# Inverting the 32-row triangles of a chunked RWKV-7 scan as two blocks of 16 at once, joined by small matmuls

## The chip, the core and the metric

The kernel is one program on one core of a Trainium2 chip. The core has five engines that run side by side, each through its own list of instructions in order: TensorE (PE, with its weight loads shown apart as PEld), VectorE (DVE), ScalarE (ACT), GpSimd (POOL) and SyncE (SP, which issues the DMAs). They wait for one another by semaphores. The metric is the device time of one execution in microseconds (us). The granted clock of TensorE is shown as a share of full speed; 1.00 is 2.4 GHz and 0.50 is 1.2 GHz.

## The reference, cut to what matters

One step of a two-layer backbone on 640 tokens (128 of a prompt, 512 of a grid) with 1024 channels. Each layer has a large input projection, an RWKV-7 branch, a gated MLP branch, an output projection and a feed-forward block. The RWKV-7 branch is a recurrence over tokens, for 16 heads of 64 channels in two directions:

```
def _rwkv_step(S, inp):
    r, w, k, v, neg_kk, b = inp
    sa = jnp.einsum('dbhij,dbhj->dbhi', S, neg_kk)
    S = S * w[..., None, :] + sa[..., :, None] * b[..., None, :] + v[..., :, None] * k[..., None, :]
    return S, jnp.einsum('dbhij,dbhj->dbhi', S, r)
```

The kernel does not step through tokens. It cuts them into 10 chunks of 64 and, within a chunk, needs the inverse of a unit triangular matrix of 64 rows whose entries are products of `neg_kk` and `b` with the decays between them. With that inverse a chunk is a handful of matmuls, and only the state goes from chunk to chunk.

## The kernel before, in words

Channels lie on partitions, tokens along the free axis. Every dense product is taken in three fp32r passes (high by high, high by low, low by high), each weight block being loaded as `raw`, rounded to `hi` by ScalarE (line 101) and subtracted to `lo` by VectorE (line 103). A dense block of 128 output channels is 48 matmuls of 128x320 in line 111; the profile counts each of them once, and each fp32 matmul twice (two passes).

Heads are handled in pairs, 8 pairs per layer (`NPAIR`), and each pair in two generators. `front(i)` prepares pair i: decays and scaled operands (`LA`, `BK`, called the scaling part below), then 40 gram matmuls `g` (line 644) whose results are copied out by ScalarE and VectorE, then 20 transposes of `BK` (line 664), then the triangular inverses, then the join of two 32-row halves to 64 rows. `back(i)` runs the chunks of pair i: 22 transposes `trv` (line 730), then 10 chunk steps of matmuls into `pu` (lines 751 to 795). While `back(i)` runs, `front(i+1)` is advanced between its steps: the table `SP['n']` says by how many yields after each of the 10 chunk steps. Dense blocks for pair i+2 (`krv_block`) and for the gates (`gate_block`) are put in between as well. The front of pair 0 has no back beside it. A scheduler then places every instruction by its own estimates and by the priorities (`high_priority`), so that the order on an engine mixes all of these.

The inverses, before: a 64-row triangle has two diagonal triangles of 32 rows. Tile `D` holds them with heads and halves on four groups of 32 partitions (quadrants) and 20 units (10 chunks, two directions) along the free axis. A 32x32 VectorE transpose (line 668) puts one triangle on each partition, as `AA`. POOL makes the unit triangle `X` of it by two selections (lines 670, 671). Then 30 steps of forward substitution follow on VectorE, each a product into scratch (line 676, written over `D`) and a sum into `X` (line 678) over (31-s)*s elements. Two transposes (lines 692, 694) give the inverse in both orientations, `XT` and `XN`; four ScalarE copies (line 698) put it into `TT`. Two groups of 40 quadrant matmuls, `pw` in lines 705 and 715, with ScalarE copies behind them (lines 709, 718), form the 32x32 block off the diagonal. `back(i)` reads `TT` in line 789.

Of the kernel before, what the change touches and what calls it, by code (L numbers as in the profile page):

```python
# [16 lines left out]
T = TP + TS  # L17
# [17 lines left out]
SP = {'n': (3, 2, 1, 2, 2, 1, 0, 0, 3, 1), 'v': 1, 'k': 4, 'r': 7, 'kk': 7, 'F': 200, 'B': None, 't': 10, 'g0': 2, 'gn': (2, 2, 2, 1, 2, 2, 2, 1)}  # L35
# [6 lines left out]
def emit(tc, I, O, depth=DEPTH, mark=lambda s: None):  # L42
    nc = tc.nc
    ctx = ExitStack()
    with ctx:
# [22 lines left out]
        for half in range(2):  # L68
# [4 lines left out]
            nc.gpsimd.affine_select(m_str[s], m_str[s], pattern=[[1, L]], compare_op=ALU.is_gt, fill=0.0, base=0, channel_multiplier=-1)  # L73
        cb = {}
# [19 lines left out]
        def dense_ps():  # L94
            return psd.tile([128, 2, 512], F32, tag="d", name="dps")
# [211 lines left out]
        for l in range(depth):  # L307
# [73 lines left out]
            with tc.tile_pool(name=f"com{l}", bufs=1) as com:  # L381
# [139 lines left out]
                with tc.tile_pool(name=f"rw{l}", bufs=1) as rw:  # L521
# [25 lines left out]

                    st_ = {}
# [33 lines left out]
                    def front(i):  # L582
# [87 lines left out]
                        nc.gpsimd.affine_select(X, AA, pattern=[[1, 32], [-1, 32]], compare_op=ALU.is_gt, fill=0.0, base=0, channel_multiplier=0)  # L670
                        nc.gpsimd.affine_select(X, X, pattern=[[1, 32], [-1, 32]], compare_op=ALU.not_equal, fill=1.0, base=0, channel_multiplier=0)  # L671
                        tm = D.rearrange("p u t -> p (u t)")
                        for s in range(1, 31):
                            n = 31 - s
                            t3 = tm[:, 0:n * s].rearrange("p (a b) -> p a b", b=s)
                            nc.vector.tensor_tensor(t3, AA[:, s + 1:32, s:s + 1].to_broadcast([128, n, s]),  # L676
                                                    X[:, s:s + 1, 0:s].to_broadcast([128, n, s]), ALU.mult)
                            nc.vector.tensor_tensor(X[:, s + 1:32, 0:s], X[:, s + 1:32, 0:s], t3, ALU.add)  # L678
                            if s % 5 == 0:
                                yield "sub"  # L680
                            if s == 10:
# [12 lines left out]
                        nc.vector.transpose(XN.rearrange("p u j -> p j u"), X.rearrange("p t j -> p j t"))
                        for q in range(4):
                            s = slice(32 * q, 32 * q + 32)
                            o = 32 * (q % 2)
                            nc.scalar.activation(TT[s, :, o:o + 32], XT[s, 0:20, :], AF.Copy)
# [379 lines left out]
```

## Time and profile before

| what | us |
|---|---|
| median of 3 runs (lowest, highest) | 3382.55 (3381.95, 3396.24) |
| the profiled execution | 3388.05 |
| its span, first to last instruction | 3386.3 |
| TensorE matmuls busy | 3159.4 (93%) |
| VectorE busy | 2145.6 (63%) |
| ScalarE busy | 1511.6 (45%) |
| GpSimd busy | 612.4 (18%) |

Per engine, busy time is the union of its instructions' times. Matmuls overlap in the array and their ends are modelled, so a busy TensorE is not one at its peak: a row with few, short matmuls at half clock is also counted as busy. A line of the kind `L676 DVE ... x480 | 178.1, 371 | 21.6 <-POOL X L671 11.7` says: line 676 on VectorE, 480 times, 178.1 us busy, 371 ns for one, 21.6 us of idle time just before them, most of it ended by GpSimd's line 671. The pairs' part of the program stands at about 300 to 1100 us (layer 0) and 1960 to 2770 us (layer 1).

### The profile page before, as it was taken

How to read it: one execution, taken by the hardware profiler on the slowest of the kernel's cores; microseconds unless marked ns; L12 is line 12 of the kernel's file. 1: busy time of each engine (PE TensorE's matmuls, PEld its weight loads, DVE VectorE, ACT ScalarE, POOL GpSimd, SP SyncE). 2: the span in 40 equal slices, each digit the busy share in tenths (PEclk: the TensorE clock that was granted, in tenths of full speed). 3: DMA queues.
4: the chain of work that ended last, by engine and by line, in shares of the span. 5: the costliest groups of instructions: out<-in, count | busy, mean ns of one | idle time of the engine just before them, and what ended most of it. 6: DMA issues, size and time to landing. Idle time of an engine off the chain costs nothing.

```text
span 3386.3 us, 66312 instructions
## 1 busy us (share of the span) xinstructions
PE 3159.4 (93%) x26160; PEld 2862.3 (85%) x26160; DVE 2145.6 (63%) x4147; ACT 1511.6 (45%) x3268; POOL 612.4 (18%) x616
## 2 busy tenths in 40 slices
PE   7998899999999999999989979999999999999998
PEld 7897677777778989999989967777777789899998
DVE  7777778887785469933353487788787735532234
ACT  5444445554445354224254434445544543541432
POOL 3004333333231000000000133333323210000000
PEclk8998889998899999999999989899889999999999
DMA  6683112221224536622344522122222245222223
GB/s 210 220 291 102 56 61 72 77 74 61 66 77 138 199 104 205 216 83 75 99 135 139 188 75 66 56 73 77 68 68 72 86 137 184 84 76 75 75 75 106
DMA packets 215671, 372.73 MB, mean 110 GB/s; under 512 B 63680, under 2 KB 72000, under 8 KB 215360
## 3 DMA queue, kind: packets, MB, share of 16 engines
q1 hardware_dynamic: 215360, 368.49, 33.8%
q8 instruction: 206, 3.38, 0.4%
q14 instruction: 105, 0.86, 0.1%
HBM read 288.41 MB, written 63.31 MB: 104 GB/s over the span
## 4 chain that ended last, share of the span: by engine, by line
PE 65%; DVE 18%; DMA 5%; issue 5%; ACT 4%; POOL 3%; SPq 1%; DVEq 0%; ACTq 0%; POOLq 0%
PE dps L111 40%; PE g L644 4%; DMA wada<-in_wada 3%; PE dps L256 3%; PE dps L491 2%; DVE X L678 2%; DVE D L676 2%; PE pu L776 2%; DVE wjunk L168 2%; PE pu L757 2%; PE pu L789 1%; PE pu L795 1%; PE pu L751 1%; DVE lo L103 1%; POOL BK L625 1%
## 5 line engine op out<-in xcount | busy, mean ns | idle before, releaser
L101 ACT ACTIVATE hi<-raw 128x512 fp32r<-128x512 f32 x630 | 397.2, 632 | 1025.6 <-PE dps L111 864.0
L103 DVE TENSOR_TENSOR lo<-raw,hi 128x512 fp32r<-128x512 f32 x550 | 392.1, 714 | 545.9 <-ACT hi L101 526.7
L111 PE MATMUL dps<-ah,hi 128*128 128x320 f32 x2768 | 686.9, 324 | 8.4 <-ACT up L468 5.4
L111 PE MATMUL dps<-ah,lo 128*128 128x320 f32 x2768 | 674.3, 321 | 14.5 <-DVE lo L103 14.5
L111 PE MATMUL dps<-al,hi 128*128 128x320 f32 x2768 | 674.9, 321 | 0.0
L111 PEld LDWEIGHTS dps<-ah,lo 128*128 128x128 f32 x2768 | 474.4, 193 | 29.5 <-DVE lo L103 16.5
L111 PEld LDWEIGHTS dps<-ah,hi 128*128 128x128 f32 x2768 | 474.2, 192 | 28.2 <-ACT up L468 6.0
L111 PEld LDWEIGHTS dps<-al,hi 128*128 128x128 f32 x2768 | 473.9, 192 | 12.7 <-issue 0.8
L168 DVE CUSTOM_DVE_ANT_0 wjunk<-wada,sc 128x1024 f32<-128x1024 f32 x176 | 220.9, 1255 | 33.2 <-DMA wada<-in_wada 30.9
L785 POOL TENSOR_TENSOR sw<-SV,wc 64x128 f32<-64x128 f32 x288 | 150.7, 523 | 439.0 <-DVE SV L803 422.5
L644 PE MATMUL g<-LA,BK 64*128 64x128 f32 x1280 | 193.6, 332 | 32.9 <-DVE LA L656 15.9
L103 POOL TENSOR_TENSOR lo<-raw,hi 128x512 fp32r<-128x512 f32 x80 | 123.2, 1540 | 543.6 <-ACT hi L101 491.8
L644 PEld LDWEIGHTS g<-LA,BK 64*128 64x128 f32 x1280 | 162.0, 226 | 64.6 <-issue 22.2
L111 PE MATMUL dps<-fh,lo 128*128 128x320 f32 x896 | 205.5, 311 | 6.2 <-DVE lo L103 6.0
L111 PE MATMUL dps<-fh,hi 128*128 128x320 f32 x896 | 204.7, 310 | 0.0
L111 PE MATMUL dps<-fl,hi 128*128 128x320 f32 x896 | 204.5, 309 | 0.0
L676 DVE TENSOR_TENSOR D<-AA,X 128x30 f32<-128x30 f32 (+14 forms) x480 | 178.1, 371 | 21.6 <-POOL X L671 11.7
L678 DVE TENSOR_TENSOR X<-X,D 128x30 f32<-128x30 f32 (+14 forms) x480 | 179.9, 375 | 11.3
L249 POOL TENSOR_TENSOR al<-nt,ah 128x320 fp32r<-128x320 f32 x24 | 25.2, 1053 | 728.1 <-ACT ah L248 727.0
L111 PEld LDWEIGHTS dps<-fh,lo 128*128 128x128 f32 x896 | 150.0, 188 | 7.9 <-DVE lo L103 7.8
L625 POOL TENSOR_TENSOR BK<-ta,cum 64x640 f32<-64x640 f32 x64 | 125.8, 1966 | 141.4 <-DVE ta L616 116.3
L111 PEld LDWEIGHTS dps<-fh,hi 128*128 128x128 f32 x896 | 150.3, 188 | 0.0
(293 smaller groups left out, 5798.1 us busy)
## 6 DMA issues: line engine op xcount, KB each, us to landing
raw<-in_w SPq DMA_DIRECT2D x280, 256.0 KB, 2.6
raw<-in_win SPq DMA_DIRECT2D x234, 256.0 KB, 2.7
wada<-in_wada SPq DMA_DIRECT2D x88, 512.0 KB, 4.1
ld<-up SPq DMA_DIRECT2D x80, 320.0 KB, 3.6
th<-ld SPq DMA_DIRECT2D x32, 320.0 KB, 2.9
ta<-ld SPq DMA_DIRECT2D x32, 320.0 KB, 3.0
gd<-spill SPq DMA_DIRECT2D x32, 320.0 KB, 2.3
raw<-in_wo SPq DMA_DIRECT2D x40, 256.0 KB, 2.6
```

Source lines behind the costliest of these rows:

```text
L101: nc.scalar.activation(hi, raw, AF.Copy)
L103: (eng or nc.vector).tensor_tensor(lo, raw, hi.bitcast(F32), ALU.subtract)
L111: nc.tensor.matmul(ps[:, n, 0:HT], w[:, k * 128:(k + 1) * 128], xk[:, n * HT:(n + 1) * HT], start=(first and k == 0 and j == 0), stop=(las ...
L168: nc.vector.tensor_tensor_reduce(junk, wt, sc_cur[0][:, v, :], 1.0, 0.0, ALU.mult, ALU.add, mods[l][:, j, v:v + 1])
L256: nc.tensor.matmul(ps[:, n, 0:HT], w[:, k * 128:(k + 1) * 128], x[:, 4 * kb + k, hs(n)], start=(kb == 0 and k == 0 and j == 0), stop=(kb = ...
L491: nc.tensor.matmul(o, x[:, k, tk * 128:(tk + 1) * 128], w[:, kk * 256:(kk + 1) * 256], start=(k == 0 and j == 0 and tk % 2 == 0), stop=(k ...
L625: nc.gpsimd.tensor_tensor(b[s, c, 1 - h, :], rt[s], e[s], ALU.mult)
L644: nc.tensor.matmul(gs[h][:, c - c0, :], b[s, c, :, :].rearrange("p x t -> p (x t)"), la[s, c, h:h + 2, :].rearrange("p x t -> p (x t)"), s ...
L676: nc.vector.tensor_tensor(t3, AA[:, s + 1:32, s:s + 1].to_broadcast([128, n, s]), X[:, s:s + 1, 0:s].to_broadcast([128, n, s]), ALU.mult)
L678: nc.vector.tensor_tensor(X[:, s + 1:32, 0:s], X[:, s + 1:32, 0:s], t3, ALU.add)
L757: nc.tensor.matmul(pu[s, d, 3, :], SV[:, us[d], h, :], GR[d][:, cs[d], h, :], start=False, stop=True, skip_group_check=True)
L785: nc.gpsimd.tensor_tensor(sw[s], SV[s, both, h, :], wcu[s, both].unsqueeze(2).to_broadcast([64, 2, L]), ALU.mult)
```

## The change

`X` becomes the triangle with its lower left 16x16 block cleared, so that its two diagonal blocks of 16 rows can be inverted side by side: a view `xb` with a dimension for the block lets one VectorE instruction work on both, and the steps run to 14 instead of 30. `X` is transposed into as before (`AA` is gone), and the scratch is a tile `tm` of its own.

The cleared block is then brought in by TensorE. `pwa` multiplies the whole triangle `D` with the first 16 columns of the inverse (80 quadrant matmuls of 32x16). VectorE masks the result to rows 16 to 31 (`low16`) and adds the identity, into `wq`, whose other 16 columns are a constant identity. Multiplying with `wq` on one side gives the inverse in one orientation, `pwt` (80 matmuls of 32x32), and on the other side in the other, `pwn` (40, two quadrants only). ScalarE copies `pwn` into `XN` and `pwt` into `TT` (twelve copies in place of four). The join to 64 rows follows as before, reading `TT` instead of `XT`. The front's yields become fewer, the table `SP['n']` follows, the `bon` part moves behind the steps, and a memory reservation is made smaller.

```
-SP = {'n': (3, 2, 1, 2, 2, 1, 0, 0, 3, 1), ...
+SP = {'n': (3, 2, 1, 2, 2, 1, 1, 1, 1, 1), ...
+        idq = G([128, 32], "idq")
+        for q in range(4):
+            nc.vector.tensor_copy(idq[32 * q:32 * q + 32, :], ident[32 * q:32 * q + 32, 32 * q:32 * q + 32])
+        low16 = G([128, 1], "low16")
+        nc.vector.tensor_reduce(low16, idq[:, 16:32], mybir.AxisListType.X, ALU.add)
...
+                    wq = rw.tile([128, 20, 32], F32, tag="wq", name="wq")
+                    nc.gpsimd.tensor_copy(wq[:, :, 16:32], idq[:, 16:32].unsqueeze(1).to_broadcast([128, 20, 16]))
...
-                        AA = rw.tile([128, 32, 32], F32, tag="s4", name="AA", bufs=3)
-                        nc.vector.transpose(AA, D.rearrange("p u t -> p t u"))
-                        X = rw.tile([128, 32, 32], F32, tag="s4", name="X", bufs=3)
...
-                        tm = D.rearrange("p u t -> p (u t)")
-                        for s in range(1, 31):
-                            n = 31 - s
-                            t3 = tm[:, 0:n * s].rearrange("p (a b) -> p a b", b=s)
-                            nc.vector.tensor_tensor(t3, AA[:, s + 1:32, s:s + 1].to_broadcast([128, n, s]),
-                                                    X[:, s:s + 1, 0:s].to_broadcast([128, n, s]), ALU.mult)
-                            nc.vector.tensor_tensor(X[:, s + 1:32, 0:s], X[:, s + 1:32, 0:s], t3, ALU.add)
-                            if s % 5 == 0:
+                        X = rw.tile([128, 33, 32], F32, tag="sX", name="X")
+                        xf = X.rearrange("p t s -> p (t s)")
+                        xa = X[:, 0:32, :]
+                        nc.vector.transpose(xa, D.rearrange("p u t -> p t u"))
+                        nc.gpsimd.memset(xa[:, 16:32, 0:16], 0.0)
...
+                        xb = xf.rearrange("p (a r) -> p a r", a=2)[:, :, 0:512].rearrange("p a (t s) -> p a t s", s=32)
+                        tm = rw.tile([128, 128], F32, tag="tm", name="tm")
+                        for s in range(1, 15):
+                            n = 15 - s
+                            t4 = tm[:, 0:2 * n * s].rearrange("p (a t s) -> p a t s", a=2, s=s)
+                            nc.vector.tensor_tensor(t4, xb[:, :, s + 1:16, s:s + 1].to_broadcast([128, 2, n, s]),
+                                                    xb[:, :, s:s + 1, 0:s].to_broadcast([128, 2, n, s]), ALU.mult)
+                            nc.vector.tensor_tensor(xb[:, :, s + 1:16, 0:s], xb[:, :, s + 1:16, 0:s], t4, ALU.add)
+                            if s % 7 == 0:
                                 yield "sub"
...
+                        quads = [slice(32 * q, 32 * q + 32) for q in range(4)]
+                        pw = psr.tile([128, 20, 16], F32, tag="g", name="pwa")
+                        for u in range(20):
+                            for s in quads:
+                                nc.tensor.matmul(pw[s, u, :], D[s, u, :], XN[s, u, 0:16], start=True, stop=True)
+                        nc.vector.scalar_tensor_tensor(wq[:, :, 0:16], pw, low16, idq[:, 0:16].unsqueeze(1).to_broadcast([128, 20, 16]), ALU.mult, ALU.add)
+                        yield "W"
+                        for x in range(2):
+                            us = slice(10 * x, 10 * x + 10)
+                            pt = psr.tile([128, 10, 32], F32, tag="g", name="pwt")
+                            pn = psr.tile([128, 10, 32], F32, tag="g", name="pwn")
+                            for u in range(10 * x, 10 * x + 10):
+                                for s in quads:
+                                    nc.tensor.matmul(pt[s, u - 10 * x, :], wq[s, u, :], XT[s, u, :], start=True, stop=True)
+                            for u in range(10 * x, 10 * x + 10):
+                                for s in quads[0::2]:
+                                    nc.tensor.matmul(pn[s, u - 10 * x, :], XT[s, u, :], wq[s, u, :], start=True, stop=True)
+                            for s in quads[0::2]:
+                                nc.scalar.activation(XN[s, us, :], pn[s], AF.Copy)
+                            for q, s in enumerate(quads):
+                                o = 32 * (q % 2)
+                                nc.scalar.activation(TT[s, us, o:o + 32], pt[s], AF.Copy)
+                        yield "V"
...
+    nc = _bacc.Bacc("TRN2", target_bir_lowering=False, num_devices=1, dynamic_dma_scratch_size=2048)
```

The new steps move instructions on every engine. Three places follow, before and then after. In these rows `dps` is a dense block (after the change its line is 116), `pu` a chunk step of `back`, `pg` and `trv` as above; a row's `x40` counts matmuls of the program, of which the trace shows two records each.

TensorE, layer 0, the join of the front of pair 0, before:

```order
L111 MATMUL dps<-ah,hi 128x320 x2
L111 MATMUL dps<-al,hi 128x320 x2
L111 MATMUL dps<-ah,lo 128x320 x2
L705 MATMUL pw<-XN,TT_2827 32x32 x40
L715 MATMUL pw_3237<-XT,XN 32x32 x20
L715 MATMUL pw_3238<-XT,XN 32x32 x20
L730 MATMUL trv<-ident,vp_2547 128x128 x4
```

And after:

```order
L116 MATMUL dps<-ah,lo 128x320 x2
L116 MATMUL dps<-ah,hi 128x320
L709 MATMUL pwa<-XN,D 32x16 x80
L116 MATMUL dps<-ah,hi 128x320
L116 MATMUL dps<-al,hi 128x320 x2
L116 MATMUL dps<-ah,lo 128x320 x2
L718 MATMUL pwt<-XT,wq 32x32 x40
L721 MATMUL pwn<-wq,XT 32x32 x20
L586 MATMUL pg<-kksq,ones_b 128x320 x2
L718 MATMUL pwt<-XT,wq 32x32 x40
L721 MATMUL pwn<-wq,XT 32x32 x20
L116 MATMUL dps<-ah,hi 128x320 x2
```

Before, 152 dense matmuls stand between the last transpose of `BK` and the first `trv`, all ahead of `pw`; after, 69 stand there, 51 of them ahead of `pwa`, and the rest of those blocks comes later, among the chunk steps of pair 0.

TensorE, layer 0, a join beside a running back, before (the rest of line 715 follows):

```order
L111 MATMUL dps<-al,hi 128x320 x2
L111 MATMUL dps<-ah,lo 128x320
L705 MATMUL pw<-XN,TT_2827 32x32 x40
L776 MATMUL pu<-SV,LA_3498 64x64 x2
L776 MATMUL pu<-SV,LA_3520 64x64 x2
L751 MATMUL pu<-LA_3498,SV 64x64 x2
L751 MATMUL pu<-LA_3520,SV 64x64 x2
L757 MATMUL pu<-GR_3564,SV 64x64 x2
L757 MATMUL pu<-GR_3654,SV 64x64 x2
L111 MATMUL dps<-ah,lo 128x320
L111 MATMUL dps<-ah,hi 128x320 x2
L715 MATMUL pw_9951<-XT,XN 32x32 x17
```

And after, the two halves of `pwt` and `pwn` of such a pair:

```order
L718 MATMUL pwt<-XT,wq 32x32 x40
L721 MATMUL pwn<-wq,XT 32x32 x20
L805 MATMUL pu<-SV,LA_3690 64x64 x2
L805 MATMUL pu<-SV,LA_3712 64x64 x2
L780 MATMUL pu<-LA_3690,SV 64x64 x2
L780 MATMUL pu<-LA_3712,SV 64x64 x2
L786 MATMUL pu<-GR_3756,SV 64x64 x2
L786 MATMUL pu<-GR_3846,SV 64x64 x2
L116 MATMUL dps<-al,hi 128x320
L718 MATMUL pwt<-XT,wq 32x32 x40
L721 MATMUL pwn<-wq,XT 32x32 x20
L818 MATMUL pu<-psb,TT_3751 64x64 x4
```

The new groups stand amid the chunk steps, three steps and more before the back ends, with one dense matmul between the two halves. `pwa` stands four dense matmuls ahead of the first `pwt`, and `pw` five behind the last `pwn`.

VectorE, layer 0, the last steps of an inverse, before (`cum`, `th`, `LA`, `BK` are the scaling part of the next front):

```order
L606 SCALAR_TENSOR_TENSOR cum<-scanm,th 128x640
L676 TENSOR_TENSOR D<-AA,X 128x58
L614 SCALAR_TENSOR_TENSOR th<-ta,kkn 128x640
L678 TENSOR_TENSOR X<-X,D 128x2x29
L628 SCALAR_TENSOR_TENSOR LA_3498<-kkn,E 64x10x64
L676 TENSOR_TENSOR D<-AA,X 128x30
L624 SCALAR_TENSOR_TENSOR BK_3499<-th,cum 64x10x64
L678 TENSOR_TENSOR X<-X,D 128x30
L624 SCALAR_TENSOR_TENSOR BK_3499<-th,cum 64x10x64
L692 STREAM_TRANSPOSE XT<-X 128x32x32
L694 STREAM_TRANSPOSE XN<-X 128x32x32
L628 SCALAR_TENSOR_TENSOR LA_3498<-kkn,E 64x10x64
```

And after:

```order
L687 TENSOR_TENSOR tm<-X 128x28
L689 TENSOR_TENSOR X<-X,tm 128x2x14
L693 STREAM_TRANSPOSE XT<-X 128x32x32
L695 STREAM_TRANSPOSE XN<-X 128x32x32
L820 COPY SV<-pu 64x2x64
L710 SCALAR_TENSOR_TENSOR wq<-pwa,low_99,idq 128x20x16
L832 TENSOR_TENSOR SV<-pu,sw 64x2x64 x2
L310 SCALAR_TENSOR_TENSOR k<-zs_596,par_170,k 128x640
L820 COPY SV<-pu 64x2x64
L108 TENSOR_TENSOR lo<-raw,hi 128x512
L832 TENSOR_TENSOR SV<-pu,sw 64x2x64 x2
```

Before, the next front's scaling part is dealt out among the last steps, ahead of `XT` and `XN`. After, the steps end while chunk steps are still to come, and the scaling part stands behind the back's end.

In four of the six pairs between the first and the last, the piece of TensorE's order from `trv` to the last transpose of `BK` reads after the change as it read before it in pair 3 of the layer (the one in the window 629.4 to 725.0): 11 dense matmuls from the first `trv` to the first `g`, and 38 from there to the last transpose.

## Rows read from the trace of the kernel before

**Rows 1.** The page's part 1 (busy us, share, instructions) and the whole chain by line.

```profile
PE 3159.4 (93%) x26160; PEld 2862.3 (85%) x26160; DVE 2145.6 (63%) x4147; ACT 1511.6 (45%) x3268; POOL 612.4 (18%) x616
by line: PE dps L111 40.5%; issue 5.2%; PE g L644 4.5%; DMA wada<-in_wada 2.9%; PE dps L256 2.6%; PE dps L491 2.2%; DVE X L678 2.2%; DVE D L676 2.1%; PE pu L776 1.9%; DVE wjunk L168 1.7%; PE pu L757 1.6%; PE pu L789 1.5%; PE pu L795 1.5%; P
```

**Rows 2.** Windows from join to join: length, busy us of each engine, PEclk, DMA.

```profile
363.10:1021.50 658.40, 613.10 (x6283) 501.26 (x6284) 513.75 (x1129) 322.00 (x863) 225.68 (x230) 0.91 0.22 68
448.70:546.60 97.90, 93.34 (x891) 75.52 (x891) 74.60 (x163) 46.27 (x125) 30.03 (x33) 0.85 0.21 64
629.40:725.00 95.60, 88.87 (x963) 72.33 (x963) 78.45 (x168) 49.14 (x130) 35.38 (x36) 0.98 0.24 74
725.00:826.70 101.70, 93.76 (x900) 76.70 (x900) 77.85 (x170) 46.76 (x125) 31.42 (x33) 0.83 0.22 67
2031.10:2690.60 659.50, 613.86 (x6281) 501.82 (x6281) 515.18 (x1128) 321.96 (x863) 223.12 (x230) 0.91 0.22 68
2115.90:2215.80 99.90, 93.97 (x893) 75.70 (x894) 75.38 (x163) 46.41 (x125) 30.32 (x34) 0.85 0.20 63
2394.20:2492.00 97.80, 89.81 (x900) 73.52 (x900) 78.01 (x170) 46.66 (x125) 31.56 (x33) 0.88 0.23 70
2492.00:2590.50 98.50, 90.49 (x879) 75.18 (x879) 76.95 (x160) 47.76 (x126) 29.67 (x32) 0.88 0.22 66
```

**Rows 3.** Matmuls of line 111 alone, in two of these windows.

```profile
629.40:725.00 95.60, 46.50 (x241) 35.86 (x241) 0.98 0.24 74
725.00:826.70 101.70, 40.17 (x204) 30.90 (x204) 0.83 0.22 67
```

**Rows 4.** Windows again: last gram matmul stage of two pairs.

```profile
656.30:685.10 28.80, 26.77 (x243) 21.58 (x242) 23.23 (x51) 16.21 (x55) 14.13 (x11) 0.94 0.23 69
744.10:790.00 45.90, 40.76 (x280) 33.34 (x281) 30.84 (x66) 17.71 (x58) 17.92 (x16) 0.63 0.19 58
```

**Rows 5.** Groups by line: the 30 steps, whole run; by shape, 363 to 1021 us.

```profile
L676 DVE TENSOR_TENSOR D<-AA,X 128x30 f32<-128x30 f32 (+14 forms) x480 | 178.1, 371 | 21.6 <-POOL X L671 11.7
L678 DVE TENSOR_TENSOR X<-X,D 128x30 f32<-128x30 f32 (+14 forms) x480 | 179.9, 375 | 11.3
L676 DVE TENSOR_TENSOR D<-AA,X 128x30 f32<-128x30 f32 x14 | 2.9, 205 | 4.9 <-POOL X L671 4.7
L676 DVE TENSOR_TENSOR D<-AA,X 128x108 f32<-128x108 f32 x14 | 4.0, 288 | 0.3
L676 DVE TENSOR_TENSOR D<-AA,X 128x240 f32<-128x240 f32 x14 | 5.8, 418 | 0.4
```

**Rows 6.** Windows, last BK transpose of front 0 to the next stage, both layers.

```profile
317.50:368.00 50.50, 31.16 (x319) 29.68 (x319) 48.48 (x85) 20.32 (x35) 15.11 (x10) 0.78 0.20 58
1985.70:2036.00 50.30, 29.96 (x319) 28.49 (x318) 48.31 (x85) 20.23 (x35) 15.02 (x10) 0.79 0.20 59
```

**Rows 7.** Timeline before that join (start, us, what, idle); waits (total, times, longest).

```profile
363.08 2.34 PE L705 MATMUL pw<-XN,TT 32*32 32x32 f32 x80 [15.48 <-DVE XN L694]
PE pw L705 <- DVE XN L694: 54.1, 16, 16.5
```

**Rows 8.** Chain of waits 600 to 730 us: start us, us, what.

```profile
608.08 0.92 PE dps L111 x5
610.28 0.38 PE pu L751 x8
611.76 2.10 PE dps L111 x13
629.42 1.45 PE pw L705 x80
```

**Rows 9.** Groups by shape: copies and the nearest VectorE read of PSUM.

```profile
L709 ACT ACTIVATE XN<-pw 32x320 f32<-32x320 f32 x64 | 27.5, 430 | 1.9 <-PE pw L705 0.8
L698 ACT ACTIVATE TT<-XT 32x640 f32<-32x640 f32 x64 | 47.0, 735 | 38.1 <-DVE XT L692 37.5
L818 DVE SCALAR_TENSOR_TENSOR yc<-pg,YD 128x320 f32<-128x320 f32 x32 | 15.2, 482 | 12.1 <-PE pg L578 12.1
```

More of the change, by code (lines that the diff above doesn't have):

```diff
@@ L34 @@
 GORD = (((0, 4), (4, 4), (8, 2)), ((0, 4), (8, 2), (4, 4)))
-SP = {'n': (3, 2, 1, 2, 2, 1, 0, 0, 3, 1), 'v': 1, 'k': 4, 'r': 7, 'kk': 7, 'F': 200, 'B': None, 't': 10, 'g0': 2, 'gn': (2, 2, 2, 1, 2, 2, 2, 1)}
+SP = {'n': (3, 2, 1, 2, 2, 1, 1, 1, 1, 1), 'v': 1, 'k': 4, 'r': 7, 'kk': 7, 'F': 200, 'B': None, 't': 10, 'g0': 2, 'gn': (2, 2, 2, 1, 2, 2, 2, 1)}
 def cidx(d, p):
@@ new lines, in front @@
+                        X = rw.tile([128, 33, 32], F32, tag="sX", name="X")
[3 more added lines that the diff above has]
+                        nc.gpsimd.memset(xa[:, 16:32, 0:16], 0.0)
+                        nc.gpsimd.affine_select(xa, xa, pattern=[[1, 32], [-1, 32]], compare_op=ALU.is_gt, fill=0.0, base=0, channel_multiplier=0)
+                        nc.gpsimd.affine_select(xa, xa, pattern=[[1, 32], [-1, 32]], compare_op=ALU.not_equal, fill=1.0, base=0, channel_multiplier=0)
@@ L691, in front @@
                         XT = rw.tile([128, 32, 32], F32, tag="s4", name="XT", bufs=3)
-                        nc.vector.transpose(XT.rearrange("p u t -> p t u"), X)
+                        nc.vector.transpose(XT.rearrange("p u t -> p t u"), xa)
                         XN = rw.tile([128, 32, 32], F32, tag="s4", name="XN", bufs=3)
[L694 to L698, printed above, removed]
@@ L699, in front @@
-                        yield "mrg"
+                        nc.vector.transpose(XN.rearrange("p u j -> p j u"), xa.rearrange("p t j -> p j t"))
+                        nc.scalar.activation(vp[1][:, 64:64 + T], v[:, ::-1], AF.Copy)
+                        bon = kd[0]
+                        nc.vector.tensor_tensor(bon, kd[0], kd[1], ALU.add)
+                        nc.vector.scalar_tensor_tensor(bon, bon, P[:, RKC + i:RKC + i + 1], r, ALU.mult, ALU.mult)
+                        ps = dense_ps()
@@ new lines, in front @@
+                        f32mm(ps, ones_b, bon)
+                        nc.vector.tensor_tensor(pv(bon), ps[:, :, 0:HT], pv(v), ALU.mult)
+                        nc.sync.dma_start(bvd[i], bon)
+                        yield "bon"
+                        quads = [slice(32 * q, 32 * q + 32) for q in range(4)]
[3 more added lines that the diff above has]
+                                nc.tensor.matmul(pw[s, u, :], D[s, u, :], XN[s, u, 0:16], start=True, stop=True)
@@ L709, in front @@
                                 nc.scalar.activation(wsb[s, 320 * x:320 * x + 320], pw[x][s].rearrange("p u t -> p (u t)"), AF.Copy)
+                        yield "mrg"
                         pw = [psr.tile([128, 10, 32], F32, tag="g", name="pw2") for _ in range(2)]
@@ L714, in front @@
                                     s = slice(64 * h + 32, 64 * h + 64)
-                                    nc.tensor.matmul(pw[x][64 * h:64 * h + 32, u - 10 * x, :], wsb[s, u * 32:(u + 1) * 32], XT[s, u, :], start=True, stop=True)
+                                    nc.tensor.matmul(pw[x][64 * h:64 * h + 32, u - 10 * x, :], wsb[s, u * 32:(u + 1) * 32], TT[s, u, 32:64], start=True, stop=True)
                             for h in range(2):
@@ L1068 @@
     arrays = prep(inputs)
-    nc = _bacc.Bacc("TRN2", target_bir_lowering=False, num_devices=1)
+    nc = _bacc.Bacc("TRN2", target_bir_lowering=False, num_devices=1, dynamic_dma_scratch_size=2048)
     I = {k: nc.dram_tensor("in_" + k, a.shape, mybir.dt.from_np(a.dtype), kind="ExternalInput").ap() for k, a in arrays.items()}
```

12 lines of the change are left out of this document (removed).

## The prediction

> **What bounds the kernel now.** I read the busy shares and the whole chain first, then windows over the pairs, then what TensorE waits for. TensorE is busy for 93% of the span, VectorE for 63%. On the chain the dense matmuls hold 40.5%, and the two lines of the inverse hold 4.3% together (2.2 and 2.1), about 146 us [rows 1]. That is the most that the inverse could be said to set. The windows tell how it sets it. From the first join of a layer to its last, seven pairs take 658.4 and 659.5 us, some 94 us each, with TensorE busy for 93% and VectorE for 78% of it, at a mean clock of 0.91 [rows 2]. A pair is not set by VectorE's sum: pair 3 (629.4 to 725.0) has the most VectorE work shown, 78.45 us, and takes 95.6 us, while 725.0 to 826.7 has 77.85 us and takes 101.7 [rows 2]. It also has more dense matmuls, 241 against 204 [rows 3]. What differs is the clock, 0.98 against 0.83; in the gram stage alone it is 0.94 against 0.63, and the stage takes 28.8 against 45.9 us [rows 4]. TensorE waits for the inverse by one row, the join `pw` on the transpose `XN`: 54.1 us in 16 waits, of which the longest is 16.5 and the one in layer 0's first front is 15.48 [rows 7]. The other 14 share 54.1 - 16.5 - 15.5 = 22.1 us, 1.6 us each. So I hold TensorE, with its clock, for the bound of the pairs beside a back, and VectorE for the bound only in the front of pair 0. There VectorE is busy for 48.5 of 50.5 us and TensorE for 31.2, at a clock of 0.78; layer 1 is the same [rows 6].
>
> **VectorE, removed.** 60 instructions per front took (178.1 + 179.9) / 16 = 22.4 us. The 28 new ones hold 28 to 112 elements, 80 in the mean. By the rows at 30 (205 ns) and 108 elements (288 ns) one takes 0.26 us, so 7.3 us; at 240 elements it is 418 ns, so halving the elements does not halve the time [rows 5]. New is one read of PSUM into `wq`, 0.48 us by its nearest row [rows 9]. VectorE gives back 14.6 us per front, 234 us of its 2145.6. Beside a back this lies beside TensorE's work, and is worth only the wait that it ends.
>
> **Term a, the front of pair 0, twice.** TensorE sits idle there for 50.5 - 31.2 = 19.3 us, and 20.3 in layer 1 [rows 6]. VectorE's 14.6 us come off the path, no more. TensorE's dense matmuls ahead of `pwa` (51 of 0.147 us, the price worked out under d) last 7.5 us, the shortened chain of steps, transposes and selections longer, so some idle stays; and 83 dense matmuls are put off, to places where they may or may not fill a gap. I take -12 us a layer, -24 in all, between -29 (all of it) and -16 (half and a little).
>
> **Term b, the other 14 waits for `XN`.** The steps now end while chunk steps of the back are still queued, so this wait goes: -22 us. If the new join meets a busy VectorE instead, half comes back: -10.
>
> **Term c, matmuls added.** 80 + 80 + 40 are 200 per front, 400 records. 80 such records of the old join took 1.45 us at full clock, 18 ns each [rows 8], and 2.34 in the first front, where the clock was low, 29 ns [rows 6, 7]. Those use two quadrants at a time. Most of the new ones are dealt over four. If four run side by side a record costs 9 ns, 3.6 us per front; if no more than two do, 7.3 us. No row shows four. I take 4.5 us, nearer to the lower end, since 160 of the 400 are half as wide: 16 x 4.5 = +72 us, between +58 and +117. TensorE is the bound here, so none of it is hidden.
>
> The Trainium skill has a rule that speaks against this term: "TensorE: Matmul & The Clock Gate", in "Wait — 56ns, not 53.3ns?", says that matmuls never start less than about 25 ns apart, however narrow. The row's mean of 18 ns is already under it, so this trace does not agree; by the page, 400 x 25 ns would be 10 us per front and the term +160, the time 3498.
>
> **Term d, changes between dense and small groups.** 13 dense matmuls take 2.10 us and 5 take 0.92 before a chunk group follows [rows 8], so one costs 1.18 / 8 = 0.147 and each change 0.92 - 0.74 = 0.18 us. Four more per front: 16 x 4 x 0.18 = +12, at best 0.
>
> **Term e, waits inside the join.** Where one wait was, there are now four: `pwt` on `wq`, the second `pwt` on a PSUM buffer, `pw` on `XN` and on a buffer, and its second half on ScalarE. Four matmuls of `pu` (8 records) take 0.38 us [rows 8]. With four dense ones they last about 1 us ahead of the first `pwt` and cover `wq`'s 0.48. Between the halves ScalarE has six copies of 430 ns [rows 9], 2.6 us, and TensorE has twelve matmuls of `pu` and one dense, some 1.2 us: 1.4 us are bare. Ahead of `pw` there are again six copies against five dense matmuls and four of `pu`, 1.1 us: 1.5 us. Ahead of the second half it is about 1.0. That is 3.9 us if each wait is met in full. Behind a waiting matmul stand the chunk steps and everything else of TensorE, so a wait here is not hidden. In part ScalarE's copies begin earlier than the group's end; I take 2.0: +32 us, between 0 and +62. ScalarE itself gains 12 x 430 - 4 x 735 ns = 2.2 us per front, and is at 49% of a pair.
>
> "TensorEngine Tiling (Array Packing)" in the Trainium skill, "PSUM Bottleneck", speaks against the change as well: packing speeds up TensorE and not the copies out of PSUM, which may become the bound. The copies' rows (5.2 us for twelve) against 4.5 us of matmuls agree as far as they go. By that rule the term would stand at its upper end, +62, and the time at 3440.
>
> **Term f, the clock.** Half clock takes 2 x (1 - 0.91) x 658 = 118 us of each layer's seven pairs, 237 in all. Five windows below 0.89 hold 29 + 35 + 30 + 23 + 24 = 141 of it [rows 2]; the other nine hold 11 each. TensorE's order from `trv` to the last transpose is after the change, in four of six pairs, that of pair 3, the cleanest. If the five become like the other nine, 141 - 54 = 87 us are run at twice the speed: -43. If all 14 become like pair 3 (3.8 us each) it is (237 - 53) / 2 = -92. But the new join is a stretch of small matmuls and waits three times as long as the old, and TensorE's clock fell where it had little to do [rows 4, 6]; 6 us at half clock in each of 14 joins would give back 42: +42. I take -43.
>
> **Sum.** -24 - 22 + 72 + 12 + 32 - 43 = +27 us on the profiled execution's 3388.05, so 3415. The runs' median stands 5.5 below that execution: 3410. The change takes work off the engine with room and puts it on the one without.
>
> **The rivals.** First, faster: the clock holds and four quadrants run at once. Deciding is the mean clock of the seven pairs: from about 0.95 on the gain is larger than the join's cost. Terms then: -24 - 22 + 58 + 12 + 10 - 92 = -58, so 3325. For it speaks that pair 3 shows such a clock with the same order; against it, that the join adds bare waits.
>
> Second, also faster: VectorE paced the pairs after all, as 78% busy and the 4.3% on the chain may be read. The steps on the chain shrink as 7.3 to 22.4, -98 us, the waits for `XN` go (-22), and c to e lie in TensorE's gaps: 3382.55 - 120 = 3263. Against it: the 14 waits are 22 us, and pair 3 against its neighbour.
>
> Third, no change: c at 58, d and e together 22, f and the rest as taken: -24 - 22 + 58 + 22 - 43 = -9, so 3374, and with e at its taken value 3396.
>
> Fourth, much slower: each new group runs as the first front's join did, at 29 ns a record [rows 7], since the clock is down whenever it comes or since each narrow record has a floor of its own. Term c is then 16 x 11.7 = 187: +115 over the forecast, so 3525. For it speaks that the new groups come with little dense work among them; against it, the 18 ns of the join at 629.42. (The page's 25 ns lies between the two rows.)
>
> That the change doesn't do what it says would be that the 14 steps cost more per element, by their four-dimensional views: 28 at 418 ns, the longest row, are 11.7 us, and VectorE still gives back 10; only term a would suffer, by some 8 us.
>
> **How the numbers follow.** My forecast, slower with a sum between +10 and +70, has 0.35 (its own range 3392 to 3450); the fourth rival 0.10; no change 0.25; the first 0.20 and the second 0.10. A measurement of this kernel can tell about 0.5%, 17 us, from no change. So slower 0.45, same 0.25, faster 0.30. The range of 8 in 10 leaves out the second and the fourth rival: 3335 to 3475.
>
> **What would show it.** Right: the seven pairs of a layer no shorter than 658 us; the row of `pw` waiting on `XN` gone but for short waits, and in its place TensorE waiting on ScalarE's copies within the new groups, 1 to 2 us each; the stage of rows 6 down from 50 to under 38 us; 28 steps in 7 to 8 us; VectorE's busy time down by about 230; the records of `pwa`, `pwt` and `pwn` at 9 to 18 ns each. Wrong: a mean clock in the pairs of 0.95 and more, or pairs under 90 us, or the 80 records of `pwt` taking over 2 us at full clock.

## The result, and the profile after

The changed kernel takes 3525.51 us (median of 4 runs, 3509.05 to 3538.75) against 3382.25 us of the kernel before on the same chip (4 runs). The ratio is 1.041, with a 95% interval of 1.036 to 1.046: slower by 143 us. The forecast was 3410, with a range of 3335 to 3475: right that it would be slower, wrong by 115 us in how much. The profiled execution took 3538.75 us, with a span of 3537.0.

Part 1 of the page and the whole chain of the kernel after, as in [rows 1]:

```profile
PE 3328.0 (94%) x32560; PEld 3010.1 (85%) x32560; DVE 1938.6 (55%) x3656; ACT 1542.6 (44%) x3396; POOL 595.1 (17%) x634
by line: PE dps L116 37.3%; issue 3.5%; PE g L652 2.9%; PE dps L261 2.8%; DMA wada<-in_wada 1.9%; PE dps L496 1.7%; PE pu L805 1.6%; DVE lo L108 1.6%; PE pu L780 1.4%; PE pu L818 1.4%; PE pu L786 1.4%; PE pu L824 1.3%; DVE wjunk L173 1.3%; 
```

VectorE lost 207 us of work, and the step lines are gone from the head of the chain. TensorE gained 169 us of busy time. Windows of the kernel after, from a layer's first join to its last (both layers), one pair, and the front of pair 0 in both layers (columns as in [rows 2]):

```profile
332.00:1058.00 726.00, 673.67 (x8953) 556.59 (x8945) 438.19 (x916) 340.94 (x920) 216.93 (x232) 0.85 0.20 63
2072.00:2812.00 740.00, 690.52 (x8976) 569.86 (x8980) 438.16 (x917) 341.16 (x920) 218.21 (x232) 0.82 0.20 62
618.80:731.10 112.30, 103.36 (x1338) 84.84 (x1342) 64.16 (x136) 50.37 (x135) 32.80 (x35) 0.85 0.20 64
320.00:348.90 28.90, 23.64 (x635) 20.96 (x633) 13.98 (x30) 15.12 (x32) 3.92 (x4) 0.82 0.18 51
2060.70:2089.00 28.30, 23.88 (x635) 21.07 (x633) 14.03 (x30) 15.01 (x32) 3.92 (x4) 0.82 0.18 53
```

Against [rows 2] the seven pairs grew from 658 to 726 and from 660 to 740 us, and their clock fell from 0.91 to 0.85 and 0.82. Against [rows 6] the front of pair 0 shrank from 50 to 29 and 28 us, as forecast. What TensorE waits for (total us, times, longest), and groups by line (count, busy us, mean ns, idle before):

```profile
PE dps L116 <- DVE lo L108: 41.8, 21, 3.2
PE pwa L709 <- DVE XN L695: 21.3, 16, 4.0
PE pwt L718 <- issue: 7.2, 8, 1.8
PE pw L733 <- ACT XN L723: 0.7, 2, 0.4
```

```profile
L687 DVE TENSOR_TENSOR tm<-X 128x28 f32<-128x28 f32 (+6 forms) x224 | 57.7, 257 | 10.2 <-POOL X L681 4.9
L689 DVE TENSOR_TENSOR X<-X,tm 128x28 f32<-128x28 f32 (+6 forms) x224 | 61.1, 273 | 6.3
L709 PE MATMUL pwa<-XN,D 32*32 32x16 f32 x2560 | 30.2, 185 | 26.3 <-DVE XN L695 21.3 <-issue 5.1
L718 PE MATMUL pwt<-XT,wq 32*32 32x32 f32 x2560 | 40.9, 229 | 7.8 <-issue 7.2 <-ACT XN L723 0.6
L721 PE MATMUL pwn<-wq,XT 32*32 32x32 f32 x1280 | 38.9, 227 | 1.0 <-issue 0.9
```

The long waits for `XN` of [rows 7] are gone: 21.3 us in 16 waits, none over 4.0. The 28 steps take (57.7 + 61.1) / 16 = 7.4 us, as [rows 5] gave. The join's three groups are busy for 110 us in all. None of this is 143 us. One account finds the rest. A run lists its span and its mean granted clock. Their product is the time that the span would have at the full level; the remainder is booked to the half level (1.2 GHz). Time in which TensorE stood idle at the half level is in that remainder too, so it says where the time lies and not what a higher clock would win back. By medians over the runs that is 3184 + 200 us before and 3221 + 303 us after: 37 us of added work, and 103 us of clock. In the profiled executions it is 3190 + 196 and 3212 + 325. In pair 3 of layer 0 the fall can be seen: 10 us ahead of `pwa`, from `pwa` to the fall, and from there until the clock rises.

```profile
608.80:618.80 10.00, 9.31 (x91) 8.06 (x90) 9.44 (x26) 3.20 (x8) 2.11 (x3) 1.00 0.31 95
618.80:625.60 6.80, 5.25 (x309) 4.58 (x309) 2.20 (x5) 1.25 (x3) 1.22 (x3) 1.00 0.18 48
625.60:649.50 23.90, 22.36 (x370) 17.65 (x369) 2.72 (x9) 10.49 (x27) 0.91 (x3) 0.50 0.04 13
```

### The profile page after: what moved, and what is told of

It reads as the page before. It is cut to its first block, busy times and chain, and to the rows that moved or that the text cites. A ratio compares the mean times of both kernels' runs of the same rounds, so it can differ in the third digit from the quotient of the medians.

```text
span 3537.0 us, 78831 instructions
## 1 busy us (share of the span) xinstructions
PE 3328.0 (94%) x32560; PEld 3010.1 (85%) x32560; DVE 1938.6 (55%) x3656; ACT 1542.6 (44%) x3396; POOL 595.1 (17%) x634
## 4 chain that ended last, share of the span: by engine, by line
PE 60%; DVE 12%; issue 4%; DMA 3%; ACT 3%; POOL 1%; SPq 0%; DVEq 0%; ACTq 0%; POOLq 0%
PE dps L116 37%; PE g L652 3%; PE dps L261 3%; DMA wada<-in_wada 2%; PE dps L496 2%; PE pu L805 2%; DVE lo L108 2%; PE pu L780 1%; PE pu L818 1%; PE pu L786 1%; PE pu L824 1%; DVE wjunk L173 1%; PE pg L586 1%; PE tr L672 1%; PE pwt L718 1%
## 5 line engine op out<-in xcount | busy, mean ns | idle before, releaser
L116 PE MATMUL dps<-ah,lo 128*128 128x320 f32 x2768 | 687.6, 326 | 35.4 <-DVE lo L108 33.8
L116 PE MATMUL dps<-ah,hi 128*128 128x320 f32 x2768 | 703.3, 330 | 6.9 <-ACT up L473 5.9
L116 PE MATMUL dps<-al,hi 128*128 128x320 f32 x2768 | 691.6, 327 | 0.0
L116 PEld LDWEIGHTS dps<-ah,lo 128*128 128x128 f32 x2768 | 483.3, 196 | 51.9 <-DVE lo L108 37.1
L116 PEld LDWEIGHTS dps<-ah,hi 128*128 128x128 f32 x2768 | 483.1, 195 | 30.2 <-ACT up L473 6.7
L116 PEld LDWEIGHTS dps<-al,hi 128*128 128x128 f32 x2768 | 481.7, 195 | 16.5 <-issue 1.2
L652 PE MATMUL g<-LA,BK 64*128 64x128 f32 x1280 | 183.2, 339 | 30.4 <-DVE LA L664 16.0
L652 PEld LDWEIGHTS g<-LA,BK 64*128 64x128 f32 x1280 | 154.7, 233 | 61.4 <-issue 19.4
L820 DVE COPY SV<-pu 64x128 f32<-64x128 f32 x160 | 46.4, 294 | 225.6 <-ACT SV L819 186.7
L116 PEld LDWEIGHTS dps<-fl,hi 128*128 128x128 f32 x896 | 151.3, 190 | 0.0
```

Of the source, the lines that this page charges most:

```text
L116: nc.tensor.matmul(ps[:, n, 0:HT], w[:, k * 128:(k + 1) * 128], xk[:, n * HT:(n + 1) * HT], start=(first and k == 0 and j == 0), stop=(las ...
L652: nc.tensor.matmul(gs[h][:, c - c0, :], b[s, c, :, :].rearrange("p x t -> p (x t)"), la[s, c, h:h + 2, :].rearrange("p x t -> p (x t)"), s ...
L820: nc.vector.tensor_copy(SV[64:128, both, 1, :], pu[64:128, :, 1, :])
```

## The experiments

Each edit below is against the changed kernel (kernel 4's against the kernel before) and is shortened. T1 and T2 are the two theories that a run was to tell apart. The same account for every kernel, in us: median time, ratio to the kernel before on the same chip, span times clock, remainder.

| kernel | time | ratio, 95% interval | at full clock | lost to half clock |
|---|---|---|---|---|
| before (runs beside 1, 5 and 8) | 3384 to 3387 | 1 | 3183 to 3184 | 197 to 200 |
| after | 3525.5 | 1.041 (1.036 to 1.046) | 3221 | 303 |
| 1, 14 steps without the join | 3380.7 | 0.998 (0.996 to 0.999) | 3170 | 206 |
| 2, dense filler in the join | 3721.6 | 1.099 (1.096 to 1.102) | 3379 | 340 |
| 3, old table | 3595.9 | 1.063 (1.060 to 1.066) | 3261 | 334 |
| 4, pair 0 only | 3370.6 | 0.995 (0.993 to 0.997) | 3193 | 179 |
| 5, hand-overs only | 3389.0 | 1.002 (0.9995 to 1.0035) | 3209 | 178 |
| 6, gate block behind the join | 3529.4 | 1.044 (1.039 to 1.049) | 3214 | 312 |
| 7, dense blocks into the join | 3490.8 | 1.033 (1.027 to 1.039) | 3247 | 243 |
| 8, the join with 30 steps | 3500.4 | 1.036 (1.032 to 1.040) | 3287 | 213 |

**1. The steps alone.**

```
-    pwa, wq, pwt, pwn and the copies out of them
+    for q, s in enumerate(quads):
+        nc.scalar.activation(TT[s, :, 32*(q%2):32*(q%2)+32], XT[s, 0:20, :], AF.Copy)
```

> The changed kernel without the join of the 16-row blocks: no pwa, wq, pwt, pwn and no copies out of them; TT is filled by four ScalarE copies of XT, as in the kernel before. The lower left 16x16 blocks of the inverses are left out. What is left of the change is 14 steps instead of 30 and the order of the work. T1 (the join's thin matmuls on TensorE are what lowers the clock, and the low clock is what costs): the time lies at or below the kernel before, 3335 to 3390 us, and the clock is at its lower level for less than 430 us in all (392 before, 648 in the changed kernel). T2 (the order of the work, or VectorE being relieved, moves the clock, and the join does not): the time stays above 3450 us with more than 550 us at the lower level.

Measured: 3380.7, 7 us under before, and 433 us at the lower level (here and below in the profiled execution, worked out from a clock listed to three decimals, so to some 3 us). T1 held on the time, and on the clock within that rounding of its bound of 430: without the join the clock stays. But it also shows how little there was to win: 210 us less on VectorE are worth 14 us of TensorE's time, since the wait for `XN` is 24.8 us where it was 54.1, and the dense matmuls' wait for `lo` is 39.4 where it was 20.6.

**8. The join alone.**

```
-    for s in range(1, 15): ... # two blocks of 16
+    for s in range(1, 31): ... # 32 rows, in place in X
-    'n': (3, 2, 1, 2, 2, 1, 1, 1, 1, 1)
+    'n': (3, 3, 2, 3, 3, 1, 1, 1, 1, 1)
```

> The changed kernel with the 30 steps of 32 rows back in the place of the 14 steps, and the join kept: the other half of the change, alone (the join works on whole inverses, so what it gives is not the reference's). VectorE has its old work, and the join's thin matmuls come as late as the merging steps did in the kernel before, with 12 dense matmuls ahead of them, 5 and 7 between. The table of steps has four more in it for the four more pauses of the 30 steps. T1 (the join lowers the clock wherever it stands): at or above 3480 us, with 550 us or more at the lower level. T2 (it lowers the clock only where it meets the thin matmuls of the state updates, as it does since VectorE is done early): the 78 us of TensorE time and little more, 3440 to 3475 us, with less than 480 us at the lower level.

Measured: 3500.4, 412 us at the lower level. On the clock T2 held. The time lies in T1's range and 25 us above T2's, but not for T1's reason: the join costs 103 us at the full clock and not 78, and it is work and not the clock that is added: 49.6 us of waits for `XN` stay, and TensorE now meets ScalarE (`pw` on `XN` 8.2 us). Put together, kernels 1 and 8 take apart the change. Steps alone: -14 work, +6 clock. Join alone: +103 and +13. Both: +37 and +103. The join fills time in which TensorE waited, and gets 52 us cheaper; the clock loses 84 us that neither half loses alone.

**5. The hand-overs without the thin matmuls.**

```
-    for u in range(20):
-        for s in quads:
-            nc.tensor.matmul(pw[s, u, :], D[s, u, :], XN[s, u, 0:16], ...)
+    for s in quads:
+        nc.tensor.matmul(pw[s], D[s, 0, :], XN[s, 0:20, 0:16], ...)   # pwt, pwn alike
```

> The changed kernel with every wait, copy and hand-over of the join kept, but with one matmul of many columns for each quadrant in the place of 40 to 80 thin ones: 4 for pwa, 4 and 2 for each half of pwt and pwn, so 16 matmul instructions for a front instead of 400 (the products are those of one head and chunk against all, so the inverses are not computed). The two merging steps pw and pw2 stay as they are, and the order of the dense matmuls too. T1 (the time that TensorE spends on thin matmuls lowers the clock): the time at the lower level falls from 648 us to below 500 us, and the time to 3380 to 3440 us. T2 (the chain of hand-overs between TensorE, VectorE and ScalarE, not the matmuls in it, is what leaves TensorE with little dense work): the time at the lower level stays above 580 us, and only the 78 us of the join's matmuls go, 3440 to 3480 us.

Measured: 3389.0, 352 us at the lower level. T1 held. The 200 thin matmuls of a front (400 records, which the expectation sets against 16) became 16 wide ones (32 records), on the same 32x32 tiles. Against kernel 1 this kernel has 39 us more at the full clock, 47 in the profiled executions, where its wide matmuls take 50 from start to start. So nothing is left that the waits and copies, which are all there, would cost. Without the many thin matmuls the clock is no lower than before, though the wide ones take 50 us where the thin ones take 78.

**2. Dense filler.**

```
+    def fill(bank, n):
+        for _ in range(n):
+            nc.tensor.matmul(bank[:, 320:512], hh[:, 0, 0:128], hh[:, 1, 0:192], ...)
     # 10 at each of: amid pwa, behind pwa, behind each pwt and pwn
```

> The changed kernel with useless dense matmuls (128x128 by 192 columns) among the join's thin ones, 60 for each front and 10 at a place, into the spare columns of the same PSUM banks: some 5 us of added TensorE work for each front at the full clock, about 80 us in all. T1 (the clock falls because the join's matmuls are thin, and dense ones among them hold it): the time at the lower level falls from 648 us to below 450 us, and the kernel is faster than the changed one in spite of the added work, 3400 to 3500 us. T2 (the clock falls for another reason): the time at the lower level stays at 600 to 700 us and the kernel is 50 to 110 us slower than the changed one, 3575 to 3635 us.

Measured: 3721.6, 196 us over the changed kernel, and 660 us at the lower level. T1 as I had put it fell. T2's price was too small as well: the filler costs 158 us at the full clock, 0.165 us each and not 0.08. Two windows of this kernel: from pair 3's `pwa` to its second `pwt`, and the 20 us from where the clock falls.

```profile
648.00:658.50 10.50, 10.49 (x413) 9.66 (x413) 2.20 (x5) 3.33 (x7) 1.21 (x3) 1.00 0.12 31
662.30:682.30 20.00, 20.00 (x254) 14.44 (x255) 1.23 (x5) 6.28 (x16) 0.79 (x2) 0.50 0.01 2
```

To the second `pwt` this pair's join, with its filler, runs at 1.00. Then the second `pwn` and the chunk steps alternate by single matmuls, the merging steps follow with ten of the fillers spread among them, and the clock is at 0.50. So in this pair the filler only put off the fall. In others it did not do that much: from `pwa` to the end of the last `pwn` and its filler the 16 joins have a mean clock of 0.78, the lowest 0.51, where the changed kernel's have 0.67.

**6 and 7. Real dense blocks moved.**

```
-                        gate(min(ng, 1))            # behind the ten steps
+                            if step == 6:  gate(min(ng, 1))    # kernel 6; step 7 in kernel 7
-    'k': 4, 'r': 7
+    'k': 5, 'r': 6                                             # kernel 7 alone
```

> The changed kernel with the first of each pair's blocks of dense gate matmuls (48 of 320 columns) issued at the pair's seventh step, where the join is, and no longer after the tenth; nothing is added or left out. T1 (it is the place of the dense matmuls against the thin ones that decides: behind the join come some 30 thin groups with 1 to 4 dense matmuls between, and there the clock stays low): the time at the lower level falls below 560 us and the kernel is 30 us or more faster than the changed one, below 3495 us. T2 (the join's thin matmuls lower the clock wherever the dense ones stand; what comes here is missing elsewhere): 600 to 700 us at the lower level, 3510 to 3560 us.

> The changed kernel with that gate block at the eighth step, and two dense blocks of the pair after next at the sixth and seventh step (fifth and eighth before), so that 23 dense matmuls stand between the join's groups and 40 or more right behind them, where the changed kernel has 20 and then groups of 1 to 4. T1 (place decides): below 540 us at the lower level, below 3480 us. T2 (the join decides): 600 to 700 us at the lower level, 3510 to 3560 us.

Kernel 6: 3529.4, 598 us at the lower level; T2's time. The gate block came behind the join's last group, and within it stood as few dense matmuls as before. In the traces the 30 us from each join's start hold 205 us at the lower level, where the changed kernel's hold 320, but the rest of the program holds 392 for 328: as T2 had it, what came here was missing elsewhere. Kernel 7: 3490.8 and 451 us. T1 held for the clock; its time missed the bound by 11 us because the order costs 26 us of work. The intervals of the ratios of kernel 7 and of the changed kernel still touch; what they lost to the clock does not, 219 to 267 us against 274 to 325 over the runs. The same join in two kernels shows it best. TensorE's timeline from pair 3's `pwa` on (start, us, what, idle before), first the changed kernel, then kernel 7:

```profile
618.81 1.76 PE L709 MATMUL pwa<-XN,D 32*32 32x16 f32 x160 [0.70 <-DVE XN L695]
620.50 0.45 PE L824 MATMUL pu<-SV,BK 128*64 128x64 f32 x8
620.88 0.56 PE L116 MATMUL dps<-ah,lo 128*128 128x320 f32 x2
...
624.10 0.79 PE L721 MATMUL pwn<-wq,XT 32*32 32x32 f32 x39
624.83 0.45 PE L805 MATMUL pu<-SV,LA 128*64 128x64 f32 x8
...
627.83 0.64 PE L116 MATMUL dps<-al,hi 128*128 128x320 f32 x1
628.39 1.29 PE L718 MATMUL pwt<-XT,wq 32*32 32x32 f32 x80
629.48 1.25 PE L721 MATMUL pwn<-wq,XT 32*32 32x32 f32 x39
...
635.99 1.28 PE L733 MATMUL pw<-XN,TT 32*32 32x32 f32 x40
637.19 0.90 PE L116 MATMUL dps<-ah,hi 128*128 128x320 f32 x2
638.02 2.35 PE L744 MATMUL pw<-TT,XN 32*32 32x32 f32 x80
...
643.88 0.69 PE L780 MATMUL pu<-LA,SV 64*64 64x64 f32 x8
644.51 0.69 PE L786 MATMUL pu<-GR,SV 128*64 128x64 f32 x8
```

```profile
625.80 1.53 PE L709 MATMUL pwa<-XN,D 32*32 32x16 f32 x160 [1.55 <-DVE XN L695]
...
628.42 0.85 PE L718 MATMUL pwt<-XT,wq 32*32 32x32 f32 x78
629.10 0.19 PE L721 MATMUL pwn<-wq,XT 32*32 32x32 f32 x1
...
630.14 0.76 PE L721 MATMUL pwn<-wq,XT 32*32 32x32 f32 x37 [0.81 <-issue]
630.83 0.41 PE L116 MATMUL dps<-ah,lo 128*128 128x320 f32 x1
...
632.54 0.31 PE L116 MATMUL dps<-ah,lo 128*128 128x320 f32 x1
632.78 0.87 PE L718 MATMUL pwt<-XT,wq 32*32 32x32 f32 x79
...
638.70 1.45 PE L744 MATMUL pw<-TT,XN 32*32 32x32 f32 x80
```

In the changed kernel one dense matmul stands between the join's two halves, and the second 80 records of `pw` take 2.35 us, a chunk group 0.69. In kernel 7 twelve stand there, and the same 80 take 1.45 us. Over 30 us from the join on, dense matmuls alone, in the changed kernel, in kernel 7 and in kernel 5:

```profile
618.80:648.80 30.00, 9.13 (x24) 5.83 (x24) 0.00 (x0) 0.00 (x0) 0.61 0.08 21
```

```profile
625.80:655.80 30.00, 14.99 (x84) 12.40 (x84) 0.00 (x0) 2.18 (x3) 1.00 0.25 81
```

```profile
602.50:632.50 30.00, 16.39 (x81) 12.18 (x82) 0.00 (x0) 1.38 (x2) 1.00 0.14 40
```

24 dense matmuls at a mean clock of 0.61 against 84 and 81 at 1.00. A count in a fixed time also falls with the clock itself, so the order has to be counted too: between pair 3's `pwa` and its last `pw` group stand 16 dense matmuls in the changed kernel, 16 in kernel 5 and 23 in kernel 7. Kernel 5 keeps the clock with 16 and without the thin ones, kernel 7 with 23 and all of the thin ones. Over all 16 joins these 30 us have a mean clock of 0.67, in kernel 7 of 0.90, in kernel 5 of 0.95.

The order alone does not settle it. In eight joins of the changed kernel TensorE has the same groups in the same order for these 30 us. Seven have a mean clock of 0.53 to 0.66; the eighth has 0.89, and no run shows why (dense matmuls alone, as above):

```profile
955.30:985.30 30.00, 12.53 (x55) 8.77 (x55) 0.00 (x0) 1.37 (x2) 0.89 0.12 34
```

**3. The old table.**

```
-    'n': (3, 2, 1, 2, 2, 1, 1, 1, 1, 1)
+    'n': (3, 2, 1, 2, 2, 1, 0, 0, 3, 1)
```

> The changed kernel with the table of dense matmuls between the fronts' steps as it stood before, (3,2,1,2,2,1,0,0,3,1) in place of (3,2,1,2,2,1,1,1,1,1): two of its dense groups come after the second join in place of one at each of two earlier steps. T1 (the dense blocks around the join bear on the clock only a little beside the join itself): within 20 us of the changed kernel, 3500 to 3545 us. T2 (the table is what moved the clock): back by 60 us or more, below 3460 us.

Measured: 3595.9, 70 us more than the changed kernel. Both theories missed. The table does not place dense blocks, as the expectation has it: it says how many pieces of the next front go out after each chunk step. The old values send out none after two late steps and three at once after the next. The kernel has 40 us more of work and 31 us more of clock. In this order `pwa` and `pu` alternate by single matmuls, as this stretch of its timeline shows.

```profile
505.25 0.33 PE L824 MATMUL pu<-SV,BK 128*64 128x64 f32 x2
505.51 0.23 PE L709 MATMUL pwa<-XN,D 32*32 32x16 f32 x2
505.67 0.33 PE L824 MATMUL pu<-SV,BK 128*64 128x64 f32 x2
505.93 0.28 PE L709 MATMUL pwa<-XN,D 32*32 32x16 f32 x2
```

Two records of `pu` take 0.26 us there (505.25 to 505.51); in the changed kernel's timeline above eight take 0.38 (620.50 to 620.88). So the new table is a part of the change that helps it.

**4. A version faster than both.**

```
+    if i == 0:  14 steps, join of 16-row blocks
+    else:       30 steps, as before                  # with the old table
```

> The new inversion for the first pair of each layer only, where TensorE waits for VectorE; the other 14 fronts keep the 30 steps and have no join of 16-row blocks; the old table. T1 (the shorter steps gain where VectorE is waited for, the join costs where TensorE sets the pace): 15 to 45 us faster than the kernel before, 3340 to 3368 us. T2 (the cost is in something done once for each layer or in the memory settings that came with the change): 3450 us or more. If the first front's join costs there what it costs in a pair, 5 to 10 us of the gain go: 3360 to 3375 us.

Measured: 3370.6 against 3387.4, 17 us faster (12 runs; ratio 0.993 to 0.997). T1 held on the gain and in its narrower range of 3360 to 3375; the wider one ended at 3368. The new inversion pays where VectorE sets the time, twice in the program, and there are only two joins to pay for. By the account the gain is in the clock, 179 us for 200, against 10 us more of work. A part of it is the front of pair 0, where TensorE sat idle at a low level [rows 6]: in layer 0 that stretch takes 28.4 us at a mean clock of 0.82, for 50.5 at 0.78. Where the rest was won is not shown.

## Why the prediction was wrong

**Front of pair 0 (a), forecast -24.** About right. The stage lost 22 us in each layer, of which part came back with the dense matmuls put off. Kernel 4, which has this term and two joins, gained 17; with 2/16 of the join's 78 us (point c) the term is about -27.

**The other waits for `XN` (b), -22.** About right: 54.1 us of waits became 21.3. In the profiled executions TensorE's time on dense matmuls, with the waits behind them, fell from 2412 to 2369 us at the full clock (from each start to the next, times the granted clock): -43 for a and b, where I had -46. But kernel 1, which has both terms and no join, gains 14 us at the full clock by the runs. In its profiled execution the dense matmuls' time falls alike, to 2365, and the chunk steps' rises by 22. What was late next, and not in my list, is `lo`: its wait rose from 20.6 to 41.8 us. Before, it was:

```profile
PE dps L111 <- DVE lo L103: 20.6, 12, 3.2
```

**Matmuls added (c), +72.** Right. Start to start at the full clock, `pwa`, `pwt` and `pwn` take 30, 26 and 22 us, 78 in all. Four quadrants do run side by side: 78 records of `pwt` in kernel 7 take 0.68 us to the next group's start, 9 ns each, half of the 18 ns of the old join's two quadrants [rows 8]. The Trainium skill ("TensorE: Matmul & The Clock Gate", "Wait — 56ns, not 53.3ns?") has matmuls start no less than about 25 ns apart; this trace does not agree.

**Changes between groups (d), +12.** Not told apart: all of TensorE's other time (merging steps, chunk steps, gram matmuls, transposes) moved by -12 us at the full clock.

**Waits inside the join (e), +32.** Wrong: next to nothing. `pw` waits for ScalarE's copies 0.7 us in all, and in kernel 5 the hand-overs leave no cost that can be measured. I had set 1.2 us of matmuls against the copies between the halves; in pair 3 3.6 us lie there (624.83 to 628.39), most of it at half clock. In kernel 8, at a higher clock, the rows of TensorE waiting on `wq` and on ScalarE's `XN` inside the join add up to 20 us (5.5, 2.4, 8.2 and 3.6). So part of this term may have been hidden by the low clock; no run shows how much.

**The clock (f), -43.** This is the step that failed: +103 by the runs' medians, +129 in the profiled execution, and with the wrong sign. I read the clock of the pairs from the order of the gram stages and held that five low stages would become like the rest. They did not: `trv`, the gram matmuls and the transposes of `BK` stand at half clock for 94 us before and for 95 after. I had also read the low clock as a sign of little to do, though TensorE counts as busy for 40.76 of 45.9 us in the low stage of [rows 4]. The price that I kept for the join, +42, was for 6 us at half clock in each of 14 joins. It is over 20 us in 12 of all 16, because the clock stays down behind the join: from the start of the join 30 us have a mean clock of 0.67 over the 16 joins, against 0.95 in kernel 5. The half-clock time rose by some 256 us in the profiled execution (start to start again). The join's own matmuls hold 71 of it; dense matmuls (+79), chunk steps (+69) and the merging steps (+25) hold most of the rest. The tax falls on the neighbours.

**The fourth rival** gave 3525, and 3525.5 came. Its number is right by accident: it priced the thin records alone at 187 us, and they took 113. The clock is not down when they come: over the 10 us ahead of `pwa` it is at 1.00 in all 16 joins, and `pwa` runs at half clock for 8.6 of its 34 us. It falls within 8 us of the join's start, and `pwt` and `pwn` run at half clock for 62 of their 79 us. Kernel 5 shows that without the thin records it stays up, in all joins but one; kernel 7 shows that it mostly stays up where more dense matmuls stand among them.

The cause is settled as far as removing either side restores the clock: the thin matmuls (5), the early steps (8), or the lack of dense work (7, in part). What of the order decides is open: kernel 2's filler did not hold the clock, and one order gave both levels. Why kernel 7 still loses 243 us and not 200 was not tried; its joins are not where it does. The 30 us from their start hold 99 us at the lower level, where those of the kernel before hold 109, and the rest of the program holds 351 for 283.

## What to carry to other kernels

Before moving work from VectorE to TensorE in small tiles, look at which matmuls stand between the small groups and just behind them. In this kernel the thin groups cost 78 us of their own at the full clock, and the half clock cost 103 us more, most of it on the work that followed them. Price the clock from a stretch with the same mixture, not from the stage that looks cleanest. And use such a trade only where the relieved engine is waited for: in two stages of this kernel it gains 17 us, in all sixteen it loses 143.

## What the runs showed of the hardware

A TensorE that counts as busy can run at half clock. In kernel 3, over 30 us from pair 3's join on, all engines (TensorE busy first):

```profile
620.90:650.90 30.00, 30.00 (x551) 23.11 (x551) 5.25 (x14) 10.41 (x25) 3.60 (x9) 0.58 0.05 11
```

Busy for 30.00 of 30.00 us, at a mean clock of 0.58. In kernel 7, over the 30 us of the same pair, it is busy for less and the clock is at 1.00:

```profile
625.80:655.80 30.00, 28.59 (x754) 24.56 (x756) 8.03 (x19) 15.68 (x34) 7.65 (x11) 1.00 0.25 81
```

So a full busy column of a profile is no sign of the full clock.

One order of instructions can settle at either level. In kernel 5 the join of pair 5, with the same groups of matmuls in the same order in both layers, has in 30 us (dense matmuls alone):

```profile
800.80:830.80 30.00, 11.42 (x29) 7.57 (x29) 0.00 (x0) 0.60 (x2) 0.50 0.03 10
2472.30:2502.30 30.00, 14.91 (x68) 10.76 (x69) 0.00 (x0) 1.39 (x2) 0.94 0.11 30
```

29 dense matmuls at 0.50 in layer 0, 68 at 0.94 in layer 1. In both the clock falls within 1 us of `pwa`; it rises again after 31 us in layer 0 and within 4 us in layer 1. What decides between the two no experiment tried.
